# A decoder trunk with routed experts: the first expert's transposed rows from one-hot products instead of a gather and transposes

## The chip, the cores and the metric

The kernel runs on one core of a Trainium2 chip. The metric is the device time of one execution in microseconds. The profile is one execution of the same program, recorded by the hardware profiler; its times count from the start of the recorded span. The engines are PE (TensorE products; PEld its weight loads), DVE (VectorE), ACT (ScalarE), POOL (GpSimd, which issues the indirect DMAs) and SP (SyncE, which issues the plain DMAs, one after the other in one queue).

## What is computed

512 tokens of width 1024 pass through two layers. Each has a mixer (layer 0 RWKV-7 and gated linear attention, layer 1 sparse attention), a norm, and a mixture of 16 experts, of which each token uses two:

```python
def _moe(h, router_w, router_bias, w_gate, w_up, w_down):
    s = jax.nn.sigmoid((hf @ router_w).astype(f32))
    sel = s + router_bias
    ...                              # best group of 4, top 2 experts in it
    gate = gate / jnp.sum(gate, -1, keepdims=True)
    for e in range(N_EXPERTS):
        he = (jax.nn.silu(hf @ w_gate[e]) * (hf @ w_up[e])) @ w_down[e]
        y = y + comb[:, e:e + 1] * he.astype(f32)
```

Every layer ends as `x <- LN(alpha*x + mixer(x)); x <- LN(alpha*x + MoE(x))`.

## The kernel before

The kernel computes only the tokens that an expert was chosen by, up to 128 a time. The normed tokens lie in four tiles of 128 (`k.h[:, i]`, the buffer `hy`) and are stored by SP to DRAM as `hD` and, as the start of the sum, `Y` (line 691). `out_proj_ln` makes the tiles in a given order; the last one's norm is put off into `rest`, ACT and POOL (lines 702 to 707).

`route` follows. DVE finds each token's two experts (`M`, 1 where chosen). PE sums `M` with a triangle into `cum`, so that `cum[:, i, e]` is the rank of a token among expert e's tokens (line 816). From the two one-hots `OH` DVE makes the ranks `rk` and eight one-hot matrices `rE` (line 835), and PE's `lists(0, 2)` turns them into lists of tokens per expert (line 841); DVE makes `tgt` of them (line 855). The gates come behind `tgt`, and `lists(2, 5)` distributes them. DVE's and POOL's order in this part is as written; the other engines' order, and which later work is pulled forward, is set by a planner with a cost model.

`moe_ln` runs the experts. `fetch(e)` gathers an expert's rows from `hD` by an indirect DMA into one of three buffers `xgs` (line 982). `turn(e)` transposes them on PE, eight transposes into two PSUM tiles `xtp` (line 994), and `split_hi_lo` (lines 63, 64) splits each into a high part `xgh` (ACT) and a low part `xgl` (DVE). `gate_up(e)` takes four chunks of weights, each cast by ACT to `wh` (line 581) and subtracted to `wl` (line 582), and forms three products per half chunk, `wh`·`xgh`, `wl`·`xgh`, `wh`·`xgl` (lines 68 to 70); ACT's sigmoid of the result (`sg`, line 1012) marks its end. `hid_t` and `down` finish the expert, and an indirect DMA adds the result to `Y`. Before the first expert stands:

```python
        fetch(0)
        fetch(1)
        further()
        turn(0)
        turn(1)
        ...
        gate_up(0)
```

`further()` is an `If` on a value read at run time (line 1053): where an expert has more than 128 tokens, it computes blocks more. The body isn't run with these inputs, but every engine reads the value and branches, and its tiles take buffers of the pools that `turn` and `gate_up` use, among them `xgh`, `xgl` and the PSUM tags. The raw weights go through a ring of buffers; four of them are the tiles `hy`, once these have been stored.

Of the kernel before, what the change touches and what calls it, by code (L numbers as in the profile page):

```python
# [10 lines left out]
F32 = mybir.dt.float32  # L11
# [4 lines left out]
ALU = mybir.AluOpType  # L16
# [4 lines left out]
P = 128  # L21
T = 512
D = 1024
NT = T // P
KC = D // P
# [740 lines left out]
def route(nc, k, rp, sm, hp, lg, rest, dbg=None):  # L766
# [53 lines left out]
    for i in range(NT):  # L820
        nc.vector.match_replace(r1[:, i], k.one, r2[:, i], 0.0)
    OH = R("roh", 2, NT, 16)
# [16 lines left out]
    def lists(a, b):  # L839
        for n in range(8):  # L840
            nc.tensor.matmul(lst[:, a:b].rearrange("p a e -> p (a e)"), E[:, n],
                             L[:, n, a:b].rearrange("p a e -> p (a e)"), start=n == 0, stop=n == 7)

    lists(0, 2)
# [78 lines left out]
def overflow_block(nc, k, I, L, xp, hp, yp, xg, tgt, gate, ex, n):  # L923
# [12 lines left out]
    gu = k.ps.tile([P, 512], F32, name="ogu", tag="pj", bufs=2)  # L936
# [32 lines left out]
def moe_ln(tc, k, I, L, w, xgp, xgs, tail, dbg):  # L969
# [3 lines left out]
    with ExitStack() as es:  # L973
# [12 lines left out]
        def turn(e):  # L986
            xg = xgs[e % 3]
            xh = xp.tile([P, KC, P], F32R, name="xgh", tag="xgh")
            xl = xp.tile([P, KC, P], F32R, name="xgl", tag="xgl")
            for hf in range(2):  # L990
                tp = k.ps.tile([P, 4, P], F32, name="xtp", tag="sm", bufs=3)
                for c in range(4):
                    cc = hf * 4 + c
                    nc.tensor.transpose(tp[:, c], xg[:, cc * P:(cc + 1) * P], k.ident)  # L994
                split_hi_lo(nc, xh[:, hf * 4:hf * 4 + 4], xl[:, hf * 4:hf * 4 + 4], tp)
            X[e] = xh, xl

# [4 lines left out]
        def gate_up(e):  # L1002
            xh, xl = X.pop(e)
            gu = k.ps.tile([P, 512], F32, name="gu", tag="pj", bufs=2)
            for j in range(4):
                wh, wl = chunk(e, j)
                for c2 in range(2):
                    c = 2 * j + c2
                    cs = slice(c2 * 512, c2 * 512 + 512)
                    mm3(nc, gu, xh[:, c], xl[:, c], wh[:, cs], wl[:, cs], c == 0, c == KC - 1)  # L1010
# [47 lines left out]
        fetch(0)  # L1058
# [3 lines left out]
        turn(1)  # L1062
# [4 lines left out]
        gate_up(0)  # L1067
# [103 lines left out]
def dsa(tc, k, I, es, weights, xt, dbg):  # L1171
# [9 lines left out]
    pool("pad").tile([P, PAD * 256], F32, name="pad")  # L1181
# [209 lines left out]
def tile_trunk(ctx, tc, I, out, dbg=None):  # L1391
    nc = tc.nc
    k = Ctx()
    k.I, k.mark = I, {}
# [11 lines left out]
def trunk(tc, ctx, k, I, out, dp, dbg):  # L1406
    nc = tc.nc
    with ExitStack() as es:
# [50 lines left out]
        def mixer_out(L, proj, to, hp, order, vec):  # L1459
# [9 lines left out]
            k.soon = soon  # L1469
            with tc.manual_schedule(engines={mybir.EngineType.DVE, mybir.EngineType.Pool}):  # L1470
# [5 lines left out]
        with ExitStack() as ex:  # L1476
            with ExitStack() as e1:
# [42 lines left out]
                nc.gpsimd.memset(xgs[0], 0.0)  # L1520
                mixer_out(0, proj, e2, pool("hTp", 1, e2), [(i, hf) for i in (2, 3, 0, 1) for hf in range(2)], xgs[1:])
# [142 lines left out]
```

## Time and profile before

| | |
|---|---|
| runs | 1025.09, 1035.18, 1042.02 us |
| median | 1035.18 us |
| profiled execution | 1036.16 us, its span 1034.4 us |
| PE busy | 912.6 us, 88% |
| DVE busy | 799.8 us, 77% |
| ACT busy | 563.8 us, 55% |
| POOL busy | 318.5 us, 31% |
| mean granted clock of PE | 0.957 of full speed |
| DMA | 174.72 MB, mean 169 GB/s |

Busy shares are means over the whole span; the two mixers, the two routers and the two expert loops have different limits. A row of the timeline gives the start in the span, the duration, the engine and line, the operation with the tiles it writes and reads, how many are merged, and in brackets the idle time before with what ended it. DMA-issuing instructions are listed under SPq and aren't counted as busy.

### The profile page before, as it was taken

Reading aid. Unit: us, or ns where it says so; the run is one execution under the profiler, and the core shown is the slowest. Engines: PE = TensorE matmul, PEld = TensorE weight load, DVE = VectorE, ACT = ScalarE, POOL = GpSimd, SP = SyncE. Lnnn points to the kernel's source line nnn. Section 1 sums busy time; section 2 is a strip of 40 time slices with the busy share of each in tenths; the row PEclk is TensorE's granted clock in tenths of the full one; section 3 lists DMA queues with packets and bytes.
Section 4 is the critical chain, followed back from the end, with each engine's and each line's share of the span. In section 5 each row is a group of like instructions: output and inputs, shape, how many; then the busy total and the mean of one; then the engine's idle time right before and its main releaser. Section 6 shows DMA issues by size and latency. Waiting matters only on the chain. (4 is left out here: it accounts for less than half of the span.)

```text
span 1034.4 us, 14255 instructions
## 1 busy us (share of the span) xinstructions
PE 912.6 (88%) x4780; PEld 694.8 (67%) x4780; DVE 799.8 (77%) x1680; ACT 563.8 (55%) x911; POOL 318.5 (31%) x237
## 2 busy tenths in 40 slices
PE   7799988997998995699999888898999849999995
PEld 5577766675776874477777658675567637777773
DVE  4637689398498667799999788499993579989887
ACT  5535474334336214488888534245663238888872
POOL 2200202013021013365656241203300335565532
PEclk9999999999999997799999989898999959999998
DMA  6223102212105387899996425101405669999833
GB/s 224 95 66 92 47 15 87 52 52 72 27 1 180 128 308 244 323 346 343 329 323 192 153 84 190 55 1 61 162 22 197 248 226 350 334 337 321 274 77 119
DMA packets 72564, 174.72 MB, mean 169 GB/s; under 512 B 24595, under 2 KB 25907, under 8 KB 72480
## 3 DMA queue, kind: packets, MB, share of 16 engines
q1 hardware_dynamic: 63840, 158.02, 43.7%
q0 software_dynamic: 8640, 15.68, 6.1%
q8 instruction: 41, 0.67, 0.3%
q14 instruction: 43, 0.35, 0.1%
HBM read 163.23 MB, written 26.21 MB: 183 GB/s over the span
## 5 line engine op out<-in xcount | busy, mean ns | idle before, releaser
L582 DVE TENSOR_TENSOR wl<-wr,wh 128x1024 fp32r<-128x1024 f32 (+1 forms) x193 | 240.3, 1264 | 40.4 <-ACT wh L581 33.0
L581 ACT CAST wh<-wr 128x1024 fp32r<-128x1024 f32 (+2 forms) x233 | 219.8, 953 | 83.0 <-PE pj L69 41.0
L582 POOL TENSOR_TENSOR wl<-wr,wh 128x1024 fp32r<-128x1024 f32 (+2 forms) x40 | 105.7, 2648 | 127.5 <-ACT wh L581 76.8
L69 PE MATMUL gu<-wl,xgh 128*128 128x512 f32 x256 | 103.4, 404 | 1.3 <-DVE wl L582 1.2
L70 PE MATMUL gu<-wh,xgl 128*128 128x512 f32 x256 | 102.6, 401 | 0.0
L68 PE MATMUL gu<-wh,xgh 128*128 128x512 f32 x256 | 102.3, 400 | 0.0
L68 PE MATMUL pj<-xh,wh 128*128 128x512 f32 x208 | 86.3, 415 | 10.0 <-ACT xh L63 7.0
L1047 POOL DMA_INDIRECT Y<-ys,rtgt x28 | 57.5, 2054 | 97.2 <-ACT ys L1043 23.2
L70 PE MATMUL pj<-xh,wl 128*128 128x512 f32 x208 | 86.0, 414 | 0.0
L69 PE MATMUL pj<-xl,wh 128*128 128x512 f32 x208 | 85.7, 412 | 0.0
L982 POOL DMA_INDIRECT xg<-hD,rtgt x32 | 49.5, 1548 | 35.4 <-PE xtp L994 14.1
L69 PEld LDWEIGHTS gu<-wl,xgh 128*128 128x128 f32 x256 | 49.0, 191 | 14.6 <-POOL wl L582 2.9
L68 PEld LDWEIGHTS gu<-wh,xgh 128*128 128x128 f32 x256 | 49.0, 191 | 10.6 <-ACT xgh L63 0.6
L64 DVE TENSOR_TENSOR xgl<-xtp,xgh 128x512 fp32r<-128x512 f32 x64 | 41.4, 681 | 17.6 <-ACT xgh L63 17.2
L70 PEld LDWEIGHTS gu<-wh,xgl 128*128 128x128 f32 x256 | 48.7, 190 | 9.2
L68 PEld LDWEIGHTS pj<-xh,wh 128*128 128x128 f32 x208 | 39.8, 192 | 20.1 <-ACT xh L63 7.0
L68 PE MATMUL yo<-wh,hth 128*128 128x512 f32 x128 | 50.7, 396 | 1.8 <-ACT hth L63 1.6
L69 PE MATMUL yo<-wl,hth 128*128 128x512 f32 x128 | 52.3, 409 | 0.0
L70 PE MATMUL yo<-wh,htl 128*128 128x512 f32 x128 | 50.3, 393 | 0.0
L994 PE MATMUL xtp<-c_ident,xg 128*128 128x128 f32 x256 | 36.5, 289 | 12.7 <-DMA xg<-hD,rtgt 6.4
L70 PE MATMUL pq<-wh,tl 128*128 128x512 f32 (+2 forms) x128 | 47.6, 372 | 0.0
L68 PE MATMUL pq<-wh,th 128*128 128x512 f32 (+2 forms) x128 | 46.8, 366 | 0.0
(422 smaller groups left out, 2189.2 us busy)
## 6 DMA issues: line engine op xcount, KB each, us to landing
wr<-in_wgu_dram SPq DMA_DIRECT2D x102, 512.0 KB, 9.2
wr<-in_wdn_dram SPq DMA_DIRECT2D x50, 512.0 KB, 12.8
wr<-in_w_dram SPq DMA_DIRECT2D x52, 256.0 KB, 2.7
wr<-in_wo_dram SPq DMA_DIRECT2D x16, 512.0 KB, 3.9
hy<-in_wgu_dram SPq DMA_DIRECT2D x15, 512.0 KB, 9.5
room<-in_wgu_dram SPq DMA_DIRECT2D x11, 512.0 KB, 5.9
hy<-in_wdn_dram SPq DMA_DIRECT2D x9, 512.0 KB, 10.9
hD<-hy SPq DMA_DIRECT2D x8, 512.0 KB, 2.7
```

What stands on the lines that cost most here:

```text
L64: nc.vector.tensor_tensor(lo, src, hi.bitcast(F32), op=ALU.subtract))
L68: nc.tensor.matmul(out, ah, bh, start=start, stop=False)
L69: nc.tensor.matmul(out, ah, bl, start=False, stop=False)
L70: return nc.tensor.matmul(out, al, bh, start=False, stop=stop)
L581: nc.scalar.copy(h[:, s], r[:, s])
L582: (lo or nc.vector).tensor_tensor(l[:, s], r[:, s], h[:, s].bitcast(F32), op=ALU.subtract)
L982: nc.gpsimd.indirect_dma_start(out=xg, out_offset=None, in_=k.hD, in_offset=bass.IndirectOffsetOnAxis(ap=tgt[:, e:e + 1], axis=0), bounds_ ...
L994: nc.tensor.transpose(tp[:, c], xg[:, cc * P:(cc + 1) * P], k.ident)
L1047: nc.gpsimd.indirect_dma_start(out=k.Y, out_offset=bass.IndirectOffsetOnAxis(ap=tgt[:, e:e + 1], axis=0), in_=ys, in_offset=None, bounds_c ...
```

## The change

`route` makes, as soon as `cum` is there, `slot0`: rank + 1 where a token goes to expert 0, else 0. Four compares of a row 0 to 127 with it give `pick`, for each tile of tokens a one-hot matrix token by rank. PE multiplies the normed tiles with them: for each 128 columns of the width, the four tiles' products add up to the transposed rows of expert 0, in two PSUM tiles `xt0`. The first half's 16 products stand ahead of `lists(0, 2)`, the second half's 16 behind it. `fetch(0)` and the transposes of `turn(0)` go; its splits read `xt0`. `turn(1)` moves into `gate_up(0)`, behind the products of the third of the four chunks. `pick` lies in the first gather buffer in layer 0 and in a tile that was only padding in layer 1. The overflow block's `ogu` takes the PSUM tag `sv` instead of `pj`, which `xt0` uses.

```diff
+    slot0 = R("rs0", NT)
+    stt(slot0, cum[:, 0:NT, 0], 1.0, M[:, :, 0], op0=ALU.add, op1=ALU.mult)
+    pick = k.pick0
+    for i in range(NT):
+        ts(pick[:, i], k.iota, slot0[:, i:i + 1], -1.0, op0=ALU.subtract, op1=ALU.is_equal)
+    k.xt0 = [k.ps.tile([P, 4, P], F32, name="xt0", tag="pj", bufs=2) for _ in range(2)]
+
+    def picked(hf):
+        return [nc.tensor.matmul(k.xt0[hf][:, n % 4], k.h[:, i, (hf * 4 + n % 4) * P:(hf * 4 + n % 4 + 1) * P], pick[:, i],
+                                 start=n == 0, stop=i == k.order[-1], skip_group_check=True)
+                for n, i in enumerate(np.repeat(k.order, 4).tolist())]
+
+    picked(0)
     OH = R("roh", 2, NT, 16)
...
-    lists(0, 2)
+    m = lists(0, 2)
+    behind(k.tc, picked(1)[0], m)
...
-    gu = k.ps.tile([P, 512], F32, name="ogu", tag="pj", bufs=2)
+    gu = k.ps.tile([P, 512], F32, name="ogu", tag="sv", bufs=2)
...
-                tp = k.ps.tile([P, 4, P], F32, name="xtp", tag="sm", bufs=3)
-                for c in range(4):
+                tp = k.xt0[hf] if e == 0 else k.ps.tile([P, 4, P], F32, name="xtp", tag="sm", bufs=3)
+                for c in range(4 if e else 0):
...
-        def gate_up(e):
+        def gate_up(e, among=(None, None)):
...
+                if j == among[0]:
+
+                    for first in among[1]():
+                        behind(tc, first, m)
...
-        fetch(0)
         fetch(1)
         further()
         turn(0)
-        turn(1)
...
-        gate_up(0)
+        gate_up(0, (2, lambda: [turn(1)]))
```

`behind(tc, a, b)` keeps a after b in the planner's order without a wait on a semaphore.

## Rows read from the trace of the kernel before

**Rows 1.** Busy time of each engine in stretches of the span. Columns: stretch, length, then busy us and instructions of PE, PEld, DVE, ACT and POOL, PE's granted clock (1 is full speed), mean busy share of the DMA engines, GB/s.

```profile
422.00:427.00 5.00, 4.68 (x21) 3.58 (x21) 2.08 (x3) 1.90 (x4) 1.43 (x2) 0.62 0.51 153
427.00:432.00 5.00, 5.00 (x23) 3.77 (x22) 4.52 (x5) 3.60 (x4) 1.59 (x3) 1.00 1.00 373
844.00:849.00 5.00, 5.00 (x21) 4.51 (x20) 3.58 (x6) 2.35 (x4) 3.47 (x3) 0.50 0.91 296
```

**Rows 2.** Timeline of layer 0's router, in order of engine: POOL's last step on the final tile and the two gathers, DVE's last replace, the ranks and the `rE`, PE's two sets of list products.

```profile
407.64 1.26 POOL L707 TENSOR_TENSOR hy<-hy,xg 128x512 f32<-128x512 f32 x1
413.02 1.24 POOL L982 DMA_INDIRECT xg<-hD,rtgt  x1 [4.12 <-DVE rden L860]
414.57 1.00 POOL L982 DMA_INDIRECT xg<-hD,rtgt  x1 [0.30 <-DVE rgf L867]
...
408.48 0.17 DVE L821 MATCH_REPLACE8 rt<-one,rt 128x16 f32<-128x16 f32 x1
409.27 0.29 DVE L830 TENSOR_TENSOR rtmp<-cum,roh 128x128 f32<-128x128 f32 x1
410.13 1.39 DVE L835 TENSOR_SCALAR rE<-iotab,rk 128x128 bf16<-128x128 bf16 x8
...
410.44 1.35 PE L841 MATMUL lst<-rL,rE 128*128 128x32 bf16 x8 [2.35 <-DVE rE L835]
415.22 0.48 PE L841 MATMUL lst<-rL,rE 128*128 128x48 bf16 x8 [3.44 <-DVE rL L867]
```

**Rows 3.** Timeline of layer 0 behind the branch: PE's transposes of experts 0 and 1, DVE's low part, the first product with it, the gather of expert 2, the first expert's sigmoid, the transposes of expert 2.

```profile
421.80 1.94 PE L994 MATMUL xtp<-c_ident,xg 128*128 128x128 f32 x8 [6.09 <-DMA xg<-hD,rtgt]
423.59 1.49 DVE L64 TENSOR_TENSOR xgl<-xtp,xgh 128x512 fp32r<-128x512 f32 x2 [3.82 <-ACT xgh L63]
424.06 0.69 PE L994 MATMUL xtp<-c_ident,xg 128*128 128x128 f32 x2 [0.32 <-DMA xg<-hD,rtgt]
425.27 0.99 POOL L982 DMA_INDIRECT xg<-hD,rtgt  x1 [9.70 <-PE xtp L994]
426.58 0.48 PE L70 MATMUL gu<-wh,xgl 128*128 128x512 f32 x1
432.19 0.39 ACT L1012 ACTIVATE sg<-gu 128x256 f32<-128x256 f32 x1 [0.33 <-PE gu L70]
436.85 1.04 PE L994 MATMUL xtp<-c_ident,xg 128*128 128x128 f32 x8
```

**Rows 4.** The same steps of layer 1 in its timeline: DVE's last replace, the second list products, the transposes, the first product with the low part, the sigmoid.

```profile
830.21 0.17 DVE L821 MATCH_REPLACE8 rt<-one,rt 128x16 f32<-128x16 f32 x1
836.96 0.48 PE L841 MATMUL lst<-rL,rE 128*128 128x48 bf16 x8 [3.44 <-DVE rL L867]
843.71 2.79 PE L994 MATMUL xtp<-c_ident,xg 128*128 128x128 f32 x12 [6.28 <-DVEq L1053]
847.87 0.78 PE L70 MATMUL gu<-wh,xgl 128*128 128x512 f32 x1
853.97 0.39 ACT L1012 ACTIVATE sg<-gu 128x256 f32<-128x256 f32 x1 [0.32 <-PE gu L70]
```

**Rows 5.** Timeline of PE elsewhere, at the full clock: eight f32 products of 128x128 by 128x128 in layer 0's mixer, and four transposes.

```profile
201.26 1.16 PE L326 MATMUL zps<-R,xbd 128*128 128x128 f32 x8
389.19 0.60 PE L657 MATMUL htp<-c_ident,hy 128*128 128x128 f32 x4
```

**Rows 6.** The branch, line 1053, on the engines' sequencers: count, duration in ns (min/median/max), first and last start in us. COMPARE_BRANCH is the branch itself, EVENT_SEMAPHORE the steps behind it. The first four and the fifth, DVE's tests ahead of its low parts, are of layer 0, the last three of layer 1.

```profile
L1053 SPq EVENT_SEMAPHORE  x9: 17/17/17, 420.3 to 423.5; - x9
L1053 SPq COMPARE_BRANCH  x1: 70/70/70, 414.6 to 414.6; - x1
L1053 PEldq EVENT_SEMAPHORE  x1: 51/51/51, 416.3 to 416.3; - x1
L1053 DVEq EVENT_SEMAPHORE  x1: 21/21/21, 417.8 to 417.8; - x1
...
L64 DVEq EVENT_SEMAPHORE  x4: 50/50/50, 420.7 to 424.5; - x4
...
L1053 SPq EVENT_SEMAPHORE  x9: 17/17/17, 838.4 to 843.4; - x9
L1053 DVEq COMPARE_BRANCH  x1: 68/68/68, 838.8 to 838.8; - x1
L1053 DVEq EVENT_SEMAPHORE  x1: 21/21/21, 843.4 to 843.4; - x1
```

**Rows 7.** Timeline of SP's queue: the first loads of weights into `hy` buffers in each layer. The duration of a merged row is from the first issue to the end of the last.

```profile
413.47 10.45 SPq L574 DMA_DIRECT2D hy<-in_wgu_dram  x3
808.66 3.03 SPq L574 DMA_DIRECT2D hy<-in_wgu_dram  x2
```

**Rows 8.** The expert loop: sigmoids of three successive experts in layer 0; ACT's first cast from an `hy` buffer in layer 1; and of the list of waits in the stretch 846 to 1010 (who waited for whom: us in total, times, longest) ACT's casts.

```profile
490.93 0.39 ACT L1012 ACTIVATE sg<-gu 128x256 f32<-128x256 f32 x1 [0.32 <-PE gu L70]
501.75 0.39 ACT L1012 ACTIVATE sg<-gu 128x256 f32<-128x256 f32 x1 [0.32 <-PE gu L70]
511.46 0.39 ACT L1012 ACTIVATE sg<-gu 128x256 f32<-128x256 f32 x1 [0.32 <-PE gu L70]
...
873.05 1.05 ACT L581 CAST wh<-hy 128x1024 fp32r<-128x1024 f32 x1
...
ACT wh L581 <- PE gu L70: 6.3, 18, 0.8
```

More of the change, by code (lines that the diff above doesn't have):

```diff
@@ L840, in lists @@
         for n in range(8):
-            nc.tensor.matmul(lst[:, a:b].rearrange("p a e -> p (a e)"), E[:, n],
+            m = nc.tensor.matmul(lst[:, a:b].rearrange("p a e -> p (a e)"), E[:, n],
                              L[:, n, a:b].rearrange("p a e -> p (a e)"), start=n == 0, stop=n == 7)
-    lists(0, 2)
+        return m
+    m = lists(0, 2)
+    behind(k.tc, picked(1)[0], m)
     cnt = K("rcnt", 16)
@@ L990, in turn @@
             for hf in range(2):
-                tp = k.ps.tile([P, 4, P], F32, name="xtp", tag="sm", bufs=3)
-                for c in range(4):
+                tp = k.xt0[hf] if e == 0 else k.ps.tile([P, 4, P], F32, name="xtp", tag="sm", bufs=3)
+                for c in range(4 if e else 0):
                     cc = hf * 4 + c
-                    nc.tensor.transpose(tp[:, c], xg[:, cc * P:(cc + 1) * P], k.ident)
+                    t = nc.tensor.transpose(tp[:, c], xg[:, cc * P:(cc + 1) * P], k.ident)
+                    if hf + c == 0:
+                        m = t
                 split_hi_lo(nc, xh[:, hf * 4:hf * 4 + 4], xl[:, hf * 4:hf * 4 + 4], tp)
             X[e] = xh, xl
+            return m if e else None
         def chunk(e, j):
@@ L1180, in dsa @@
     at, sm, wk, cst = pool("da", 2), pool("ds", 2), pool("dw", 2), pool("dc")
-    pool("pad").tile([P, PAD * 256], F32, name="pad")
+    k.pick0 = pool("pad").tile([P, PAD * 256], F32, name="pick0").rearrange("p (i t) -> p i t", i=NT)
     w = weights()
@@ L1393, in tile_trunk @@
     k = Ctx()
-    k.I, k.mark = I, {}
+    k.I, k.mark, k.tc = I, {}, tc
     k.ps = ctx.enter_context(tc.tile_pool(name="ps", bufs=1, space=PSUM))
@@ L1469, in mixer_out @@
             k.soon = soon
+            k.order = [i for i, hf in order if hf]
             with tc.manual_schedule(engines={mybir.EngineType.DVE, mybir.EngineType.Pool}):
@@ L1520, in trunk @@
                 nc.gpsimd.memset(xgs[0], 0.0)
+                k.pick0 = xgs[0][:, 0:NT * P].rearrange("p (i t) -> p i t", i=NT)
                 mixer_out(0, proj, e2, pool("hTp", 1, e2), [(i, hf) for i in (2, 3, 0, 1) for hf in range(2)], xgs[1:])
```

2 lines of the change are left out of this document (1 added, 1 removed).

## The prediction

> **What bounds the kernel now.** I read the page first: PE is the busiest engine, but its busy digits fall to 5, 6 and 4 in two places, and both are the stretch between a layer's router and its first expert. So I read the timeline there, engine by engine. In layer 0 PE has 0.48 us of list products at 415.22 and nothing more until 421.80, where eight transposes start; the bracket of that row gives 6.09 us of waiting, ended by the gather's landing [rows 2, 3]. Layer 1 has the same hole, 6.28 us before 843.71, but there the row names DVE's own branch, line 1053 [rows 4]. That second releaser is the reason not to book the whole hole as gain. The `If` for overflowing experts stands between the router and `turn(0)`, every engine passes it, and tiles allocated after it (`xgh`, `xgl`, and before the change `xtp`) share buffers with tiles inside it, so their writers wait until other engines are through. The rows of line 1053 show how long that takes: SP compares at 414.6 and does its first step behind the branch at 420.3, its last at 423.5; in layer 1 DVE compares at 838.8 and is through at 843.4 [rows 6]. DVE's tests ahead of the first `xgl` subtraction run from 420.7 [rows 6].
>
> Next I asked whether an earlier start survives to the end. Behind the start, experts follow each other at 9.7 to 10.8 us, read from the sigmoids [rows 8]. In the waits from 846 on, ACT's casts are released by PE freeing a pair, 6.3 us in 18 waits [rows 8], and no wait for a weight load stands in that list. An `hy` buffer loaded at 808.66 is cast from 873.05 on [rows 7, 8]. So the expert loop is a circle of PE, ACT and DVE, not a queue behind DMA: what the first expert's gate and up products gain, the layer gains.
>
> **The change, part by part, layer 0.** All times are those of the profiled execution.
>
> *DVE.* One small operation on `cum` (at most the 0.29 of line 830) and four 128x128 compares. The nearest rows are line 835, 1.39/8 = 0.17 in bf16, and line 830, 0.29 in f32 [rows 2]; I take 0.23, between them, since the compare is f32 but has one tensor input. That is 0.29 + 4 x 0.23 = 1.2 us (1.0 to 1.45), all on the router's chain: `OH`, the ranks and the eight `rE` come 1.2 later.
>
> *First half of the products.* The picks start at 408.65 (408.48 + 0.17) and end at 409.9; POOL's last step on the final tile ends at 408.9, so it doesn't hold them [rows 2]. PE starts near 409.6. Price of a product: eight f32 128x128 products take 1.16 us at the full clock, four transposes 0.60 [rows 5]; both come to about 0.11 apart. Eight transposes at the half clock take 1.94 [rows 3], 0.24 each, and the clock is half here. 16 x 0.24 = 3.8, so 409.6 to 413.5 (411.5 if the clock were full). `lists(0, 2)` stands behind them in PE's queue and waits: its last operand would be there at 411.5 + 1.2 = 412.7, it ends at 414.0 instead of 411.8. That is +2.2, of which 1.2 is DVE's and 1.0 PE's. Waiting behind it are `tgt`, the gathers and the whole gate chain, which DVE runs after `tgt` in a fixed order.
>
> *POOL and gathers.* One gather goes. The gather of expert 1 is then first: 413.02 + 2.2 = 415.2, landing 8.7 to 9.5 later as the two of before did (413.02 to 421.8; 414.57 to 424.06), at 424 to 425 [rows 2, 3]. It is needed behind chunk 2, near 427: hidden by three chunks of products. The gather of expert 2 was issued at 425.27, behind POOL's own exit, and its transposes came at 436.85 [rows 3]; 11.6 us against some 9 leaves about 2.5 us of cover, plus up to 1 for an earlier exit. A start earlier by more than that would be stopped there.
>
> *Second half, lists, branch.* The other 16 products run 414.0 to 417.9, in time in which PE waited before. `lists(2, 5)`, ready at 415.2 + 2.2 = 417.4, ends at 418.4 against 415.7: +2.7. PE is through the branch 0.6 later (415.7 to 416.3 before [rows 2, 6]), at 419.0, and ACT casts `xgh`, at 419.6 and 420.2. The eight transposes of `turn(0)`, 1.9 us on the path, are gone; so is their landing.
>
> *The low part.* DVE is through at 417.8 + 2.7 = 420.5. SP is the doubt. Two loads into `hy` stand ahead of its branch (413.47 and the next [rows 7]); these buffers are the normed tiles, now read by the second half, and SP issues in order. If the two stay ahead, SP waits for its tiles' eight products, 415.9, and compares near 416.6 instead of 414.6; with the same 5.7 us it is through at 422.3. The first subtraction (0.7) ends near 423.1, and the first product with `xgl`, at 426.58 before, starts at 423.2. From there to the sigmoid it was 5.6 us (432.19) [rows 3]; now `turn(1)` stands among it, 8 x 0.11 = 0.9 at the full clock. 423.2 + 5.6 + 0.9 = 429.7: **2.5 us gained**. Bounds: SP's branch ahead of all `hy` loads gives the subtraction at 420.9 and 4.0; all four loads ahead of it (products done 417.9, through at 424.6) give 0.3.
>
> *Clock.* Granted clock was 0.62 over 422:427 and full in 427:432, after PE had restarted at 421.80 [rows 1, 3]. In the change PE is busy from 409.6 with one short gap, so I take the full clock from 420; if it stays half until 424, some eight products cost 0.2 more, 1.6 us.
>
> **Layer 1.** The same steps lie 21.7 us plus 400 later: the last replace is at 830.21, `lists(2, 5)` at 836.96 [rows 4]. So +2.4, then `lists(2, 5)` ends at 840.3 (837.4), DVE compares at 838.8 + 2.9 = 841.7 and is through at 842.3 if it takes layer 0's 0.6, at 846.4 if it takes the 4.7 of this layer again [rows 6]. SP was through at 843.4 and holds `hy` loads too (808.66 before [rows 7]). I take 845, in between: first low-part product 845.8 against 847.87, sigmoid 845.8 + 6.5 = 852.3 against 853.97 [rows 4]. **1.7 us gained**, 0.3 to 3.2; part of it because the clock was half until 849 [rows 1].
>
> *Loads.* Four `hy` loads move behind the products, 2 of them by 10 us in layer 0 and up to 30 in layer 1. Their cover is the 64 us between load and cast, of which 34 stay [rows 7, 8]; without it 4 x 512 KB at the 373 GB/s of 427:432 [rows 1] would cost 5.6 us. Costed at nothing. In layer 0 the picks lie in gather buffer 0, whose next writer, the gather of expert 3, comes behind the branch: nothing. `ogu` in another bank is inside the `If`, which isn't run.
>
> Sum: 2.5 + 1.7 = **4.2 us (0.6 to 7.2)**. The profiled execution is 1036.16, 1.0 above the median of the runs; 1036.2 - 4.2 = 1032.0, as a median **1031**.
>
> **The rivals.** *The branch takes the gather's place* (1035): both late ends come true, 0.6 gained. For it: SP's 5.7 and DVE's 4.7 us, and SP's in-order queue. Against: the two stalls hit different engines in the two layers. The Trainium skill (Runtime: NRT & Kernel Launch, Instruction fetch mechanics) says that a taken branch to a target outside the resident instructions waits for a fetch; the trace agrees in 5.7 us, and by it the stall stays whatever the data do, which is this rival's 1035.
>
> *The expert loop settles into another order* (slower, 1039). The planner lays out all 16 experts from its own clock, and the start it plans from changes. Layer 0 has both 10.82 and 9.71 between neighbours [rows 8]. If one layer's 14 steady steps each became 0.56 longer, 7.8 - 4.2 = +3.6. It decides from 0.3 us a step. The same mechanism the other way: 1023.
>
> *Products at four passes* (slower, 1038). 23 instructions of mostly 512 columns take 5.00 us at the full clock [rows 1], so 0.054 per 128 columns; four passes are 0.22, at the half clock 0.43. Then each half takes 3.1 longer, `lists(2, 5)` ends 424.5 and 846.5, and the sigmoids come at 433.9 and 855.2 or later: +2.9. The 1.16 for eight speaks against it. The Trainium skill (FP8 and Floating Point Precision, TensorE Precision Notes) says that true FP32 takes four passes; the row, 0.11 apart, shows half of that.
>
> **How the numbers follow.** Forecast (1028 to 1034) 0.43; branch (1034 to 1036) 0.25; loop slower (1036 to 1047) 0.15; loop faster (1020 to 1028) 0.13; four passes 0.04. The runs of before spread from 1025 to 1042, which adds some 3 us to a median. 1021 to 1041 leaves out the outer parts of the loop's two cases. Two per cent, 20.7 us, is about what a measurement of this kernel can tell from no change; only both layers' loops moving together reach it: faster 0.03, slower 0.04, the same 0.93.
>
> **What would show it.** PE with 16 f32 products from about 409.6 and 16 from 414, 0.24 apart or less; `lists(0, 2)` ending 2 us later; one gather before the `If`; SP and DVE past line 1053 near 422 and 845; the first `gu` products near 420 and 842; the first sigmoids at 429.7 and 852.3 (the second with layer 0's gain taken off too); the steps between sigmoids as before. Wrong it would be by a loop with another step, by a branch that costs 5 us on an engine where it cost 0.6, or by DVE delaying more than the rows say.

## The result and the profile after

The change made the kernel slower: ratio 1.0130 [1.0104, 1.0156] from 19 runs of each, medians 1034.98 us before and 1044.79 after (1037.41 to 1052.57). (A ratio leaves disturbed runs out, and compares only runs made beside each other, so it isn't the quotient of two medians.) The forecast was 1031, with a range of 1021 to 1041, and with a chance of 0.93 no difference above 2%. The difference is under 2%, but the time lies outside the range and on the other side of no change.

The profiled execution of after took 1039.18 us, span 1037.4, only 3.0 more than before's. That pair misleads: in it layer 0's expert loop, first to last sigmoid, took 143.6 us against 153.4 before, and the same kernel run once more took 149.4. So two executions of one kernel differ by 5.8 us in this loop alone. What stayed in these two is the start of each layer's experts (28.1 and 27.8 us in layer 0, 29.9 and 30.0 in layer 1), so that is what I compare below: from the end of DVE's last replace to the start of the first expert's sigmoid. Before it is 23.5 us in layer 0 and 23.6 in layer 1 [rows 2 to 4]; after it is 28.1 and 29.9. Together 10.9 us lost, where 4.2 were to be gained.

Timeline of after, layer 0, PE, DVE, ACT and SP's loads:

```profile
408.90 0.87 DVE L828 TENSOR_SCALAR xg<-c_iota,rs 128x128 f32<-128x128 f32 x4
...
409.73 6.66 PE L832 MATMUL xt<-xg,hy 128*128 128x128 f32 x32 [1.56 <-DVE xg L828]
...
411.06 1.39 DVE L850 TENSOR_SCALAR rE<-iotab,rk 128x128 bf16<-128x128 bf16 x8
...
416.22 0.35 PE L856 MATMUL lst<-rL,rE 128*128 128x32 bf16 x8
416.42 3.82 PE L832 MATMUL xt<-xg,hy 128*128 128x128 f32 x32
...
417.59 2.12 SPq L574 DMA_DIRECT2D hy<-in_wgu_dram  x3
...
420.08 0.36 PE L856 MATMUL lst<-rL,rE 128*128 128x48 bf16 x8
...
427.23 1.29 DVE L64 TENSOR_TENSOR xgl<-xt,xgh 128x512 fp32r<-128x512 f32 x2 [3.80 <-SPq L1077]
...
427.97 0.79 PE L68 MATMUL gu<-wh,xgh 128*128 128x512 f32 x1 [7.53 <-DVE xgl L64]
...
428.99 0.63 PE L70 MATMUL gu<-wh,xgl 128*128 128x512 f32 x1
...
436.88 0.38 ACT L1036 ACTIVATE sg<-gu 128x256 f32<-128x256 f32 x1 [0.23 <-PE gu L70]
```

The 16 products of a half are recorded as x32 and take 6.66 us; `lists(0, 2)` stands behind them till 416.6 (411.8 before [rows 2]). The second half ends at 420.2 and the last lists at 420.4, and PE then has nothing until 427.97, 7.53 us. The row of the subtraction `xgl` names who was late: SP on its way through the branch, line 1077. SP had first issued three loads into `hy`, at 417.59, 418.48 and 419.38, as the products released the tiles.

After, layer 0, the branch on the sequencers (count, duration in ns, first and last start), and the issue of the last load ahead of it (KB, us to landing):

```profile
L1077 SPq EVENT_SEMAPHORE  x9: 17/17/17, 426.4 to 427.1; - x9
L1077 SPq COMPARE_BRANCH  x1: 70/70/70, 419.8 to 419.8; - x1
...
L1077 DVEq EVENT_SEMAPHORE  x1: 21/21/21, 422.6 to 422.6; - x1
```

```profile
hy<-in_wgu_dram SPq DMA_DIRECT2D x1, 512.0 KB, 7.2
```

SP's compare moved from 414.6 to 419.8, its last step from 423.5 to 427.1 [rows 6]. The load issued at 419.38 landed 7.2 later, at 426.6; SP's first step behind the branch, at 426.4, came just ahead of that, 6.65 behind the compare. Windows of after (us, then busy time and count of PE, PEld, DVE, ACT and POOL, granted clock, DMA share, GB/s):

```profile
409.00:416.00 7.00, 6.28 (x31) 6.31 (x32) 3.76 (x20) 0.16 (x1) 0.00 (x0) 0.52 0.89 313
416.00:420.00 4.00, 4.00 (x44) 3.99 (x43) 2.25 (x11) 0.77 (x3) 1.24 (x1) 1.00 0.61 194
421.00:428.00 7.00, 0.03 (x1) 0.03 (x1) 2.55 (x10) 1.07 (x2) 0.96 (x1) 0.61 0.59 210
428.00:432.00 4.00, 4.00 (x10) 3.13 (x11) 4.00 (x5) 1.05 (x1) 1.30 (x1) 0.50 0.94 316
```

The products do bring PE to its full level, 2.4 GHz (clock 1.00), but only for the second half; in the hole behind it the clock falls, and the first expert starts at 0.50, 1.2 GHz.

Timeline of after, layer 1, and its branch:

```profile
824.00 3.39 DVE L828 TENSOR_SCALAR pick<-c_iota,rs 128x128 f32<-128x128 f32 x4
...
824.13 2.73 POOL L1574 MEMSET xg<- 128x1024 f32 x3
...
827.08 6.21 PE L832 MATMUL xt<-pick,hy 128*128 128x128 f32 x32 [3.74 <-DVE pick L828]
...
837.18 0.33 SPq L574 DMA_DIRECT2D wr<-in_wgu_dram  x1
...
844.62 1.29 DVE L64 TENSOR_TENSOR xgl<-xt,xgh 128x512 fp32r<-128x512 f32 x2 [3.82 <-DVEq L1077]
...
853.83 0.39 ACT L1036 ACTIVATE sg<-gu 128x256 f32<-128x256 f32 x1 [0.24 <-PE gu L70]
```

```profile
L1077 SPq EVENT_SEMAPHORE  x9: 17/17/17, 838.5 to 845.5; - x9
...
L1077 SPq COMPARE_BRANCH  x1: 68/68/68, 838.0 to 838.0; - x1
L1077 DVEq COMPARE_BRANCH  x1: 68/68/68, 839.2 to 839.2; - x1
...
L1077 DVEq EVENT_SEMAPHORE  x1: 21/21/21, 844.3 to 844.3; - x1
```

Here the four compares take 3.39 us, while POOL clears the gather buffers beside them, and two engines leave the branch late: SP at 845.5 and DVE at 844.3. The row of `xgl` names DVE; the subtraction starts at 844.62, before SP's last step. But the last of SP's steps that it does wait for came at 844.0, so SP alone would have held it almost as long.

### The profile page after: what moved, and what is told of

Same layout as the page of the kernel before. It is cut to its first block, busy times and chain, and to the rows that moved or that the text cites. A ratio compares the mean times of both kernels' runs of the same rounds, so it can differ in the third digit from the quotient of the medians.

```text
span 1037.4 us, 14487 instructions
## 1 busy us (share of the span) xinstructions
PE 923.2 (89%) x4892; PEld 707.9 (68%) x4892; DVE 792.5 (76%) x1690; ACT 562.4 (54%) x911; POOL 309.1 (30%) x235
## 5 line engine op out<-in xcount | busy, mean ns | idle before, releaser
L582 DVE TENSOR_TENSOR wl<-wr,wh 128x1024 fp32r<-128x1024 f32 (+1 forms) x193 | 229.0, 1206 | 44.6 <-ACT wh L581 37.1
L1071 POOL DMA_INDIRECT Y<-ys,rtgt x28 | 52.5, 1876 | 82.0 <-ACT wh L581 22.5
L64 DVE TENSOR_TENSOR xgl<-xtp,xgh 128x512 fp32r<-128x512 f32 x60 | 38.4, 679 | 13.6 <-ACT xgh L63 13.6
L70 PEld LDWEIGHTS pj<-xh,wl 128*128 128x128 f32 x208 | 39.9, 192 | 10.1 <-issue 2.0
L69 PEld LDWEIGHTS pj<-xl,wh 128*128 128x128 f32 x208 | 39.8, 191 | 9.9 <-issue 1.8
```

Of the source, the lines that this page charges most:

```text
L64: nc.vector.tensor_tensor(lo, src, hi.bitcast(F32), op=ALU.subtract))
L69: nc.tensor.matmul(out, ah, bl, start=False, stop=False)
L70: return nc.tensor.matmul(out, al, bh, start=False, stop=stop)
L582: (lo or nc.vector).tensor_tensor(l[:, s], r[:, s], h[:, s].bitcast(F32), op=ALU.subtract)
L1071: nc.gpsimd.indirect_dma_start(out=k.Y, out_offset=bass.IndirectOffsetOnAxis(ap=tgt[:, e:e + 1], axis=0), in_=ys, in_offset=None, bounds_c ...
```

## The experiments

Starts are measured as above; "sum" is the two together against before's 47.1.

| kernel | layer 0 | layer 1 | sum | ratio to before |
|---|---|---|---|---|
| after | 28.1 | 29.9 | +10.9 | 1.0130 [1.0104, 1.0156] |
| picks_off_pad | 28.6 | 28.2 | +9.7 | 1.0128 [1.0059, 1.0197] |
| held_behind_branch | 24.4 | 21.3 | -1.4 | 1.0012 [0.9975, 1.0048] |
| cheap_products | 27.6 | 27.5 | +7.9 | 1.0118 [1.0051, 1.0185] |
| change_without_branch | 22.2 | 23.7 | -1.2 | 0.9992 [0.9956, 1.0027] |
| before_held | 22.2 | 24.6 | -0.4 | 0.9989 [0.9941, 1.0037] |
| held_cheap_products | 20.7 | 19.3 | -7.1 | 0.9941 [0.9889, 0.9993] |
| before_without_branch | 23.9 | 20.9 | -2.3 | 0.9953 [0.9901, 1.0006] |
| held_picks_in_pad | 24.6 | 28.2 | +5.7 | 1.0077 [1.0036, 1.0118] |
| held_busy_before_products | 20.8 | 20.1 | -6.2 | 0.9966 [0.9931, 1.0000] |
| before_held_busy | 20.6 | 24.5 | -2.1 | 0.9966 [0.9933, 0.9999] |
| held_in_layer_0 | 24.5 | 28.2 | +5.6 | 1.0127 [1.0088, 1.0165] |
| held_in_layer_1 | 28.0 | 27.3 | +8.1 | 1.0142 [1.0069, 1.0215] |
| change_again | 27.8 | 30.0 | +10.7 | 1.0102 [1.0043, 1.0161] |
| held_1_with_hint | 28.1 | 21.3 | +2.2 | 1.0032 [0.9983, 1.0080] |
| hint_and_busy | 20.8 | 19.9 | -6.4 | 1.0019 [0.9975, 1.0063] |
| before_hint_and_busy | 20.1 | 24.7 | -2.3 | 1.0061 [1.0013, 1.0110] |

All kernels with a sum of 5 or more are slower beyond their interval; the six others that are the change with a cure lie between 0.9941 and 1.0032. How those six order is more than the times can tell, so there I go by the traces. The start isn't all of the time, though: before_hint_and_busy is slower beyond its interval with a sum of -2.3. And in the six cured kernels layer 1's loop, first to last sigmoid, took 149.5 to 152.5 us, against 148.0 to 148.8 in the five traces with the gather (before and its variants) and 148.3 to 149.6 in the other seven of the change. So a part of a shorter start, up to 4.5 us, may be lost again there; that is one trace each, and no run looks for the cause.

**Which loads: the pad's or the queue's? (picks_off_pad, held_behind_branch)** In layer 1 the one-hots lie in `pad`, which the weight ring takes later. The first kernel puts them in a buffer of the norm's vectors:

```diff
-    k.pick0 = pool("pad").tile([P, PAD * 256], F32, name="pick0").rearrange(...)
+    pool("pad").tile([P, PAD * 256], F32, name="pad")
...
+                k.pick0 = lnv[0][:, 0:NT * P].rearrange("p (i t) -> p i t", i=NT)
```

> The change, with one edit: in layer 1 the four one-hots lie in the first half of ln1g, which is read for the last time just before, and not in the tile called pad. Theory of the held loads: the weight ring of layer 1 is laid over pad once the mixer is closed, so in the change its eighth load waits for the last product and the ten loads behind it with it (they went out at 784 to 808 us before the change, at 837 to 851 with it), and the expert loop of layer 1 then lives from hand to mouth (328 GB/s in it against 285). It expects these loads back at 780 to 805, under 300 GB/s in the loop of layer 1, no weight load in the chain of waits there, layer 1's first sigmoid some 2 us earlier because two loads fewer stand ahead of SP's branch, and a median of 1037 to 1040. Rival, the lead of the loads is not needed (the 64 us of cover in the prediction): the loads go back, and the median stays at 1043 to 1045.

The second also places the loads that must wait for the products behind the first expert's subtraction in the planner's order, without a wait on it, so that SP issues them behind the branch (in layer 0 from 419.17 on) and goes through it without them:

```diff
+        if self.n in self.hold:
+            behind(self.tc, ld, self.past)
...
+                w.past = low if e == 0 else w.past
...
+        w.hold = range(24, 40) if L == 0 else [*range(19, 23), *range(25, 40)]
```

> As the run before in this call, and besides, the loads that wait for the products (into the normed tiles) and those of the ring's second turn are ordered behind the first expert's low part, so that none of them stands in SP's queue ahead of its branch. Theory of SP's queue: in the change three loads into the normed tiles wait for products, SP compares at 419.75 in place of 414.6, and can't finish its steps behind the branch before the last of those loads has landed (426.6 in layer 0, 845.4 in layer 1); the first low part waits for SP's last step. It expects SP's compare at 413.7 to 415 and 831 to 833, its last step at 420 to 421 and 838 or earlier, the first gate and up product at 423.5 (422.6, when DVE is through, and 0.7 of subtraction) against 427.97, and in layer 1 no gain or at most 1 us, because DVE is through its own branch only at 844.3. Median 3 to 6 below the run before it. Rival, the branch's 6 us are code being fetched, whatever SP has in its queue: the compare is early and the last step stays near 420 or later by the same 6 us, and the first product still comes by 424; if DVE or ACT then wait for something else up to 427, the theory of SP's queue is wrong.

Timeline and window of picks_off_pad, layer 1:

```profile
794.86 0.33 SPq L574 DMA_DIRECT2D wr<-in_wgu_dram  x1
...
841.78 0.88 DVE L828 TENSOR_SCALAR ln1g<-c_iota,rs 128x128 f32<-128x128 f32 x4
```

```profile
870.00:1018.00 148.00, 141.60 (x669) 110.62 (x669) 134.10 (x147) 125.71 (x173) 86.37 (x40) 1.00 0.85 294
```

The lead came back: the loads into the ring, of which the change issued all but two at 837 or later, run from 794.86, and the DMA share in the loop is 0.85. In after it was 0.95, in before 0.83 (windows of after, then of before):

```profile
854.00:1004.00 150.00, 142.85 (x674) 111.37 (x673) 134.09 (x148) 126.23 (x174) 84.78 (x40) 1.00 0.95 328
```

```profile
854.00:1004.00 150.00, 144.04 (x680) 112.63 (x678) 134.82 (x150) 126.90 (x176) 85.35 (x40) 1.00 0.83 283
```

The time didn't follow: 1.0128. So the lost lead costs nothing that can be measured; the only gain is 2.5 us in the compares (0.88 for 3.39), as the memsets start 9.8 us ahead of them. Holding the loads, on the other hand, took out nearly all. Held_behind_branch, the branch of layer 0, then the two rows of DVE in layer 1; behind them the timeline of layer 0:

```profile
L1080 SPq EVENT_SEMAPHORE  x9: 17/17/17, 418.4 to 419.0; - x9
L1080 SPq COMPARE_BRANCH  x1: 70/70/70, 413.7 to 413.7; - x1
...
L1080 DVEq EVENT_SEMAPHORE  x1: 21/21/21, 422.5 to 422.5; - x1
...
L1080 DVEq COMPARE_BRANCH  x1: 68/68/68, 845.1 to 845.1; - x1
L1080 DVEq EVENT_SEMAPHORE  x1: 21/21/21, 845.6 to 845.6; - x1
```

```profile
423.94 0.80 PE L68 MATMUL gu<-wh,xgh 128*128 128x512 f32 x1 [3.65 <-DVE xgl L64]
...
433.05 0.39 ACT L1039 ACTIVATE sg<-gu 128x256 f32<-128x256 f32 x1 [0.24 <-PE gu L70]
```

SP is out at 419.0, 8 us earlier than in after, and the start is 4.2 us shorter than in picks_off_pad; DVE, at 422.5, is the late one now, since its lists wait for the products. Layer 1, where at most 1 us was expected, came 6.9 us earlier than in picks_off_pad: there DVE's step behind its branch took 0.6 us (845.1 to 845.6) and not 6.2, of which more below.

**What a product costs (cheap_products, held_cheap_products)** The products read only the upper half of each word, so the rows lose mantissa. The second kernel adds the hold and the moved one-hots.

```diff
+    top = lambda z: z.bitcast(BF16).rearrange("p (t b) -> p t b", b=2)[:, :, 1]
-        return [nc.tensor.matmul(k.xt0[hf][:, n % 4], k.h[:, i, ...], pick[:, i],
+        return [nc.tensor.matmul(k.xt0[hf][:, n % 4], top(k.h[:, i, ...]), top(pick[:, i]),
```

> The change, but the 32 products read only the upper two bytes of each f32 element of the normed tiles and of the one-hots, as bf16: the rows of expert 0 are truncated to bf16, so a part of the computation's precision is left out; number, shape and place of the products stay. Theory of the price: an f32 product of 128 columns cost 0.42 us at the half clock where 0.24 was forecast; a bf16 product costs 0.11 or less there, so the first half takes 1.8 in place of 6.7 us, the first lists end at 413 in place of 416.6, the second lists at 416.6 in place of 420.4, SP compares by 417, and the first sigmoid comes 3 to 5 us earlier (432 to 434 against 436.9); the same in layer 1, up to the 844.3 of DVE's branch. Median 1037 to 1041. Rival, the products' price is hidden by the branch and by the waiting loads: lists earlier by 3 to 4, first sigmoid within 1 of the change's, median 1043 to 1045.

> As held_behind_branch (loads behind the branch, layer 1's one-hots in ln1g), and the products read the upper two bytes only, as in cheap_products: expert 0's rows are truncated to bf16. Theory of the price: with SP's queue out of the way the list products and DVE's branch behind them are last (DVE through at 422.5 and 845.6), and they come 3.8 us earlier with products at a quarter of the price or less; the first sigmoid comes 24.5 - 3.8 = 20.7 us behind the last replace in layer 0 and 17.5 in layer 1 (24.5 and 21.3 with f32 products), and the median is 1027 to 1030. Rival, code being fetched or the weights' casts set the first expert's start by then: first sigmoids 23 or more and 21 behind the last replace, median 1033 to 1036.

Timeline of cheap_products, layer 0:

```profile
409.08 1.86 PE L834 MATMUL xt<-xg,hy 128*128 128x128 bf16 x16 [1.46 <-DVE xg L828]
...
426.36 0.79 PE L68 MATMUL gu<-wh,xgh 128*128 128x512 f32 x1 [10.28 <-DVE xgl L64]
```

```profile
L1079 SPq EVENT_SEMAPHORE  x9: 17/17/17, 420.1 to 425.5; - x9
L1079 SPq COMPARE_BRANCH  x1: 70/70/70, 414.9 to 414.9; - x1
```

16 bf16 products are recorded as x16 and take 0.116 each; 16 f32 ones as x32 and 0.42 each at the half clock (6.66/16), 0.24 at the full one (3.82/16). An f32 product leaves two records. With cheap products alone the start stays at 27.6: PE waits 10.28 us instead of 7.53 for the same SP. The three loads no longer wait long for the products, and SP compares at 414.9, as early as before the change; but the last load, issued at 414.23, lands at 424.94, and of SP's steps behind the branch all but the first (420.1) come at 424.96 or later. So here it is the landing that holds SP. Only with SP out of the way is the price felt: sums of -7.1 against -1.4, 5.7 us in the two starts.

**How much is the branch? (change_without_branch, before_without_branch, before_held)** The block that isn't run is left out of the program, in the change and in the kernel before; the third is before with the same hold of the loads.

```diff
-        further()
```

> The change without the If for overflowing experts (its body isn't entered with these inputs; the kernel could not treat an expert with more than 128 rows). Theory, the branch is what stands between the products and the first expert: from the casts at 421 and 422 on nothing waits, PE has no hole of 7 us at 421 to 428 and keeps the full clock that the products brought, the first sigmoid comes at 428 to 430 (436.9 in the change) and, in layer 1, 7 to 9 us earlier; median 1025 to 1032. Rival, the first expert's products wait for its weights' casts or for the second expert's gather anyway: first sigmoid at 434 or later, median 1038 or more.

> The kernel before without the If for overflowing experts (body not entered with these inputs; it could not treat an expert with more than 128 rows). It says what the gather itself costs when no branch stands beside it. Theory, the branch hides what the products save: here the gather's landing (421.8 in layer 0, 8.8 us behind its issue) still holds the transposes, so the first sigmoids come at most 1 us earlier in layer 0 and 1 to 2 us in layer 1, median 1032 to 1034, 2 to 4 above the change without branch (1030). Rival, the branch alone is the 5 us that the change without it gained: median 1030 or less here too, and the products are worth nothing even with no branch.

> The kernel before, with the loads into the normed tiles and those of the ring's second turn ordered behind the first expert's low part, as in the run held_behind_branch. It is the control of that run, whose 10 us against the change could also be a gift of the order of loads that has nothing to do with the products. Theory of SP's queue: before the change SP's last step (423.5) was hardly later than the gather's landing and the transposes behind it (421.8 to 423.7), and in layer 1 DVE's own branch ended at the same time as SP's (843.4), so the same edit gains 0 to 1 us: median 1033 to 1036. Rival, the order of loads is a gain by itself: 1030 or less, and then the products still cost 5 us or more against it.

Without the branch the change starts at 22.2 and 23.7, together 45.9, before at 23.9 and 20.9, 44.8. In layer 0 the products are 1.7 ahead; in layer 1 they are 2.8 behind, and 2.5 of that are its compares, which ran beside the memsets as in after (3.4 us for 0.9). So without a branch the products at their real price gain some 1.5 us of the two starts, as an estimate, and the times, 0.9992 and 0.9953 with overlapping intervals, don't show even that. Before without the branch, 1024.64 us, came out well below the expected 1032 to 1034. Holding the loads does nothing measurable for before (0.9989), whose loads ahead of the branch wait for no product.

**The one-hots beside the memsets (held_picks_in_pad)** Loads held as above, but the one-hots in `pad`.

> As held_behind_branch, but layer 1's one-hots lie in the tile pad, as in the change. It parts the two edits of that run. Theory, the order of SP's queue is all: median 1035 to 1037, with the eleven loads of layer 1 late as in the change (DMA over 320 GB/s in layer 1's loop) at no cost, and two loads that wait for pad or the lists ahead of SP's branch in layer 1, so a first sigmoid there some 2 to 6 us later than with the picks in ln1g. Rival, the late loads cost once the start is no longer late: median 1039 or more, with a weight load in the chain of waits of layer 1's loop. Besides, in the change two of the four compares of layer 1 took 2.9 and 2.8 us in place of 0.28, beside three memsets of POOL (824.13, 2.73 us); where the memsets fall beside the compares here too, they take as long again, whatever tile is written.

Layer 0 stays short (24.6), layer 1 goes from 21.3 to 28.2. The compares took 3.37 us again, 2.5 of the 6.9 lost. The rest is SP: the loads into `pad`'s part of the ring, which the hold doesn't cover, now wait for the products and stand ahead of the branch (`wr` at 847.15 and 847.58); SP's last step came at 853.9, and `xgl` at 853.97.

**Layer 1's two late ends (held_in_layer_0, held_in_layer_1)** The hold in one layer only, the one-hots out of `pad` in both.

```diff
-        w.hold = range(24, 40) if L == 0 else [*range(19, 23), *range(25, 40)]
+        w.hold = range(24, 40) if L == 0 else ()          # held_in_layer_0
+        w.hold = () if L == 0 else [*range(19, 23), *range(25, 40)]   # held_in_layer_1
```

> The change with layer 1's one-hots in ln1g (as picks_off_pad) and the loads ordered behind the branch in layer 0 alone. Together with the next run it splits the 10 us between the change and held_behind_branch by layer. Theory of SP's queue, as the traces so far read: layer 0 gains 3.7 (28.1 to 24.4 us from the last replace to the first sigmoid) and layer 1 stays as in picks_off_pad (28.2), since DVE's own 5 to 6 us behind its branch there (844.3, 860.2) have to do with the loads in front of the branch too: median 1039 to 1042. Rival, DVE's step behind its branch in layer 1 (0.5 us in held_behind_branch) depends on the code's place and not on the loads of that layer: it is short here too, layer 1's start is 22 to 24 and the median 1035 to 1037.

> The change with layer 1's one-hots in ln1g and the loads ordered behind the branch in layer 1 alone. Theory of SP's queue: layer 0 stays at 28 us from the last replace to the first sigmoid, layer 1 comes to 21 to 22, DVE's step behind its branch 0.5 to 1 us after its compare; median 1036 to 1039. Rival (code's place): layer 1 at 26 to 28 with 5 to 6 us at DVE's branch, median 1042 to 1045.

Layer 1's branch, held_in_layer_0, then held_in_layer_1:

```profile
L1080 SPq EVENT_SEMAPHORE  x9: 17/17/17, 845.1 to 852.8; - x9
...
L1080 DVEq COMPARE_BRANCH  x1: 68/68/68, 846.7 to 846.7; - x1
...
L1080 DVEq EVENT_SEMAPHORE  x1: 21/21/21, 847.3 to 847.3; - x1
```

```profile
L1080 SPq EVENT_SEMAPHORE  x9: 17/17/17, 836.0 to 836.6; - x9
...
L1080 DVEq COMPARE_BRANCH  x1: 68/68/68, 842.7 to 842.7; - x1
...
L1080 DVEq EVENT_SEMAPHORE  x1: 21/21/21, 848.3 to 848.3; - x1
```

With SP late and DVE through in 0.6 the start is 28.2, and the steps of SP, not DVE, come last ahead of `xgl` (852.85); with SP early and DVE 5.6 on its way it is 27.3; with both short (held_behind_branch) 21.3. Either suffices for the loss, and a cure of one alone shows next to nothing. DVE's step was short in held_in_layer_0, which leaves layer 1's loads as in picks_off_pad, where it was long; so those loads don't set it. That the shifted place of the code does is the nearest reading, but no run isolates it.

**A hint for DVE (held_1_with_hint), and the change repeated (change_again)** DVE is told of the coming branch behind the eight `rE`, as PE and SP already are.

```diff
+        made = ts(E[:, n], k.iotab, rk[:, n // NT, n % NT], None, op0=ALU.is_equal)
+    k.soon(mybir.EngineType.DVE, made)
```

> As held_in_layer_1 (the change, layer 1's one-hots in ln1g, loads ordered behind the branch in layer 1), and DVE too gets a hint of the branch, behind its eight compares for the ranks, as PE and SP have one. Theory of fetched code: DVE's first step behind the branch in layer 1 comes 0.5 to 1 us after its compare in place of 5.6, the first sigmoid 21 to 22.5 us behind the last replace in place of 27.3; layer 0 stays at 28 (SP there); time 4 to 6 below held_in_layer_1, were it run beside it: 1 to 1.5% below change_again in this call. Rival, the 5.6 us are a wait for another engine: the hint changes nothing, layer 1 at 26 to 28.

> The change itself, as the measure for the others of this call. Theory: 28 and 28 to 30 us from the last replace to the first sigmoids, two compares of layer 1 at 2.8 us or so beside POOL's memsets, eight weight loads of layer 1 held until the products; ratio to before 1.010 to 1.016 whatever the chip. Rival: the profile of the change was a chance; starts differ by over 2 us from 28.1 and 29.9.

DVE's step in layer 1, held_1_with_hint, then before_hint_and_busy, which has the same line:

```profile
L1081 DVEq COMPARE_BRANCH  x1: 74/74/74, 846.8 to 846.8; - x1
...
L1081 DVEq EVENT_SEMAPHORE  x1: 21/21/21, 847.3 to 847.3; - x1
```

```profile
L1063 DVEq COMPARE_BRANCH  x1: 74/74/74, 836.6 to 836.6; - x1
...
L1063 DVEq EVENT_SEMAPHORE  x1: 21/21/21, 842.5 to 842.5; - x1
```

In the first the step is 0.6 instead of 5.6, and layer 1 starts at 21.3 (the time is 0.7% below change_again's, where 1 to 1.5% were expected); in the second it is 6.0 in spite of the hint. The change run again gave the same starts within 0.4 us and the same step of DVE, 5.0, so the step belongs to the kernel and not to the single execution. So whether the hint helped or the place of the code that it shifted stays open.

**Keeping PE at work (held_busy_before_products, before_held_busy, hint_and_busy, before_hint_and_busy)** Products of the identity with itself fill PE's hole ahead of the products and behind the lists; their result is not used. Before gets 8 and 12 of them behind its two lists.

```diff
+    asked = busy(18, k.asked)
...
+    m = busy(4, k.ranked)
+    behind(k.tc, picked(0)[0], m)
...
+    m = lists(2, 5)
+    for _ in range(4): ...            # ident x ident
```

> As held_behind_branch, and PE is kept at work ahead of the products: 18 products of the identity with itself (f32, 128x128) behind the last logits, where PE had nothing for 5.5 us (402.0 to 407.5), 4 between the rank sums and the first product, and 4 behind the last lists; their results are overwritten or never read. It parts the two factors of a product's price, passes and clock. Theory of the clock: the first 16 products cost 0.42 us apiece only because the granted clock was 0.50 there; kept at work, PE keeps the full clock, a product costs the 0.24 that it cost in the second half, the first half takes 3.8 us in place of 6.5, the lists and DVE's branch come 2.5 to 3 us earlier in each layer, the first gate and up products of layer 0 are no longer at half the clock (2 us more), and the median is 1027 to 1031. Rival, the extra products don't hold the clock, or the work in front only moves its fall: the first half takes 6 us or more, median 1034 to 1038.

> The control of the run beside it: before_held, with PE kept at work in its hole between the lists and the transposes: 8 products of the identity with itself behind the first lists, 12 behind the last, results never read. Theory: the clock is up again when the gather lands (transposes 1.0 us for eight in place of 1.9, gate and up products of the first expert at 0.23 in place of 0.43 for some eight or nine of them), so the first sigmoid comes 2 to 3 us earlier in layer 0 (19 to 20 us behind the last replace in place of 22.2) and 1 to 2 in layer 1, where half of the wait is DVE's branch: median 1028 to 1031, and then products and gather are worth the same with PE at work too. Rival, PE's extra work delays its own branch and ACT's casts behind it: median 1033 or more.

> held_busy_before_products with DVE's hint as well: the change with all that was found taken away, its products at the full clock, SP's queue empty at the branch, no memset beside the compares. DVE's step was short there already (0.5 us), so theory: the same within 2 us, first sigmoids 20 to 21 and 20 us behind the last replace, ratio 0.993 to 0.999. Rival: the hint itself costs (a fetch that collides with the weight loads): 3 us or more slower than that.

> The same cures for the kernel before (loads behind the branch, PE at work between the lists and the transposes, DVE's hint), with the gather and the transposes as they were. Theory of fetched code: layer 1's first sigmoid no longer waits for DVE's branch (849.6 in before_held_busy, 5.9 us after its compare) but for the gather's landing, some 9 us behind its issue, 20 to 22 us behind the last replace in place of 24.5; layer 0 stays at 20.6; ratio 0.990 to 0.996, so that gather and products are level within 3 us. Rival: layer 1 stays at 24 or more.

Timeline and two windows of held_busy_before_products, layer 0, and the window of held_behind_branch, where PE came out of the hole:

```profile
411.54 3.81 PE L844 MATMUL xt<-xg,hy 128*128 128x128 f32 x32 [0.59 <-DVE xg L842]
```

```profile
411.00:415.00 4.00, 3.46 (x31) 3.49 (x32) 3.57 (x19) 0.00 (x0) 0.00 (x0) 1.00 0.82 283
423.00:427.00 4.00, 3.96 (x10) 3.13 (x11) 4.00 (x5) 1.05 (x1) 1.04 (x1) 0.57 0.97 336
```

```profile
410.00:414.00 4.00, 4.00 (x20) 4.00 (x20) 2.67 (x15) 0.00 (x0) 0.00 (x0) 0.50 1.00 344
```

The first half takes 3.81 us for 6.62 in held_behind_branch, and the start 20.8 for 24.4. The other half of the expectation, the first expert's products at the full clock, failed: behind the lists PE pauses for 2.66 us again, and the clock is 0.57 in the 4 us that follow. Before, treated alike, gets to 20.6 in layer 0 too. In layer 1 the change is 4.4 to 4.8 us ahead; before's DVE takes 5.9 through the branch there and the change's 0.6. Yet the times are 0.9966 for both, and 1.0019 beside 1.0061 with the hint, intervals overlapping. No version of the change that keeps its precision is shown to beat the kernel before: the lowest upper end is 1.0000. Held_cheap_products, which leaves part of the mantissa out, ends at 0.9993, and before_held_busy, without the products, at 0.9999.

## Why the prediction was wrong, point by point

- **Price of a product: the step that failed first.** I read the x8 of [rows 5] as eight products, 0.11 apart; they were four, as the kernel's loop at line 326 shows, 0.22 apart with two records each. The transposes that seemed to confirm it leave one record and cost half a product, so they were no price for one. With 0.42 for 0.24 at the half clock the first half took 6.7 us for 3.8, and `lists(0, 2)` ended at 416.6 for 414.0, `lists(2, 5)` at 420.4 for 418.4. The second half's forecast of 3.9 us came true (3.82) by luck: the price was nearly twice as high as I took it, and the clock was full where I took half. The four-pass rival had the price right (0.22 and 0.43, chance 0.04). The Trainium skill (FP8 and Floating Point Precision, TensorE Precision Notes), which I let the row overrule, says four passes; the trace agrees: four times the 0.054 of a single pass of 128 columns [rows 1] is 0.22, beside 0.24 measured.
- **SP: the step that cost most in layer 0.** I had two loads ahead of the branch, SP's compare at 416.6 and, 5.7 us later, its first step at 422.3 as the release of `xgl`. There were three loads, and they waited for dearer products, so that SP compared at 419.75: 3.15 late. The first step came 6.65 behind the compare, another 0.95. And the release is the last step, not the first: 427.1, with `xgl` at 427.23, another 0.7. (Before the change the rows couldn't tell: `xgl` begins at 423.59 [rows 3], 0.1 behind SP's last step at 423.5 [rows 6], but its row names ACT's `xgh`, its own input, which ended at 423.56.) Nor can one delay stand for compare to last step, since there are two parts. The first step came 4.5 to 7.0 us behind the compare in layer 0 of all sixteen traces with the branch, and 0.5 in layer 1, whatever loads stood ahead; no run shows what holds it. The steps behind the first come no earlier than the landings of the loads issued ahead of the branch. Before, layer 0: first step 420.3, landing 413.94 + 9.5 = 423.4, last step 423.5 [rows 6]. Before, layer 1: 837.50 + 5.6 = 843.1, and the step that waits for it at 843.1, the last at 843.4 [rows 6]. After, layer 1: 837.60 + 7.8 = 845.4, last step 845.5. Cheap_products, layer 0: 424.94, and the second step at 424.96. In after's layer 0 the landing, 426.6, came after the first step, 426.4, and cost hardly anything by itself. So a load ahead of the branch can hold SP in two ways: SP compares only when the products have let the load go out, and isn't through before it has landed.
- **DVE's added work.** Near in layer 0: counted from the last replace, the chain is 0.85 later (`rE` at 411.06 for 410.13 [rows 2]; forecast 1.2, 1.0 to 1.45). Wrong in layer 1, where four compares took 3.39 beside POOL's memsets. The Trainium skill (SBUF — State Buffer, Who interferes with whom) says that DVE, in its two-port mode, and GpSimd exclude each other at a shared pair of ports; the trace agrees: two of the four compares took 2.94 and 2.80 us while the memsets ran, side by side, and the other two, behind the last memset, 0.27.
- **DVE in layer 1's branch.** I took 845, between a step of 0.6 and one of 4.7; after had 5.0, at 844.3. That the two times are close is chance, since after's layer began 6.5 us earlier: from the last replace it is 20.4 us for a forecast 14.6, as the compares, the lists and the step were all later. That the step takes 0.6 to 6.2 among these kernels I didn't see; what decides is open.
- **Clock.** "Full from 420" failed: the hole at the branch, 7.5 us, gave it back, and from the first `gu` product to the sigmoid it took 8.9 us, with the clock at 0.50 in 428:432.
- **Sum.** Layer 0: sigmoid 436.9 for 429.7. Of the 7.2, 5.8 lie ahead of the first product with `xgl` (428.99 for 423.2), and 1.4 behind it (7.9 for 6.5), at the half clock. Layer 1, from the last replace: the second lists end at +13.5 for +9.9 (2.5 the compares, 1.1 the products), the sigmoid comes at +29.9 for +21.9; the 4.4 between are DVE at the branch, with SP close behind it, and the half clock that follows.
- **Right:** the gather of expert 1 was hidden, and `turn(1)` cost 0.8 us behind the third chunk (forecast 0.9); the loads' lost lead cost nothing that can be measured (picks_off_pad). Layer 0's loop got no longer in any trace (143.6 to 153.4 us, before 153.4), and layer 1's by 1.7 at most in the change itself (149.6 and 149.3 for 148.0).
- **Rivals and range.** "The branch takes the gather's place" (0.25) was the mechanism, SP in layer 0 and DVE in layer 1, but priced as a gain lost, 1035. It and the four passes stood as alternatives; both came, and the second made the first dearer, since the products hold back SP's loads and DVE's lists. The range ended at 1041 because no case added them.

## What to carry to other kernels

Ask of every added reader of a buffer which queued load must now wait for it, and what stands behind that load in its queue; here that chain (products, loads, branch, low part) cost as much in layer 0 as the products' price: 4.2 us came back by holding the loads, and 3.7 more by cheap products. Price an operation by a row whose number of instructions you know from the code, not by the count in the record. Where two engines can each be late at one join, take both away before you call either harmless.

## What the hardware showed that I had not expected

- An f32 product of 128x128 by 128 columns leaves two records and takes 0.24 us at the full and 0.42 at the half clock; a bf16 one leaves one record and takes 0.116 at the half clock; an f32 transpose leaves one and takes 0.24 at the half clock (1.94 for eight [rows 3]).
- SP, which issues the loads, was not through behind the branch before the loads that it had issued ahead of it had landed (845.4 and 845.5; 423.4 and 423.5; 424.94 and 425.5). Its first step behind the branch came 4.5 to 7.0 us after its compare in layer 0 and 0.5 in layer 1.
- DVE's way through the branch of layer 1 took 0.6, 2.4 or 4.7 to 6.2 us, by kernel. The Trainium skill (Runtime: NRT & Kernel Launch, Instruction fetch mechanics) says that a taken branch out of the resident instructions waits for a fetch; the long ways fit that, but no run here shows the fetch itself, nor what decides.
- Behind 7.5 us in which PE had nothing, its granted clock was 0.50, after 1.00 ahead of them; PE kept at work through the router was granted 1.00, and behind a pause of 2.66 us 0.57.
